# Combined weights of the output projection made on VectorE during the attention heads, and their raw buffers opened earlier

## The chip, the core and the metric

The kernel runs on one core of one Trainium2 chip. A core has a matrix engine (TensorE, PE in the profile, with its weight loads in a row of their own, PEld), a vector engine (VectorE, DVE), an activation engine (ScalarE, ACT), a general engine (GpSimd, POOL) and a queue engine (SyncE, SP), which in this kernel issues nearly all DMAs. Each engine runs its own instructions strictly in the order in which the program lists them; engines wait for one another through semaphores, and a DMA is waited for in the same way. The metric is the device time of one execution in microseconds: the median of three runs of the kernel before is 2246.56 us (2246.27 to 2248.82).

## What is computed

One decoder layer for 1024 prompt tokens behind 16 meta tokens, and for 8 samples of 4 new tokens, each with 1024 cached tokens in pages of 128. All arithmetic is float32. Cut to what matters here:

```python
h = rms_norm(x, norm_pre_g)
u = h @ w_in                                  # 2048 -> 7184 columns, split:
sq, sk, sv, sg, gq, gk, gv, gg, ga = split(u)
o_sb  = stick_breaking_attention(sq, sk, sv)  # 8 heads of 128
o_gla = gated_linear_attention(gq, gk, gv, log_sigmoid(ga @ w_alpha + b_alpha) / 16)   # 4 heads
mixed = concat([o_sb * silu(sg), rms_norm(o_gla) * silu(gg)])    # 2048 columns
y = x + rms_norm(mixed @ w_out, norm_post_g)
```

The samples go through the same layer; their stick-breaking scores run over the cached keys and values (`cache_k`, `cache_v`, found by `page_table`).

## The kernel before

**Matrix products.** A float32 operand is split into a high part (`act.copy` to the float32r type) and a low part (`vec.tensor_tensor` subtract), and each product is three matmuls: high by high, high by low, low by high. `inproj` (lines 279 to 295) makes one block of 128 columns of `h @ w_in`: eight weight chunks of 256 rows, each a DMA into a raw tile `wr`, a ScalarE cast to `wh` and a VectorE subtraction to `wl` (line 185), in buffers of the pool `wp`, three each; then three ranges of tokens with six matmuls each (lines 289 to 291).

**Order of the work.** The program is written out as one stream of projections. Everything else is cut into generators that a `Weaver` holds (lines 51 to 79): after each token range of a chunk `inproj` calls `W.beat()`, and each generator whose delay is over emits its next piece and says after how many beats it wants to go on. So one projection is 24 beats. The planner of the framework then lists each engine's instructions; those made under `urgent()` (weight chunks, evictions) are put ahead as far as their buffers allow. `spread` (line 389) keeps an instruction behind the latest matmul at the time of its beat.

**The stages,** in the order of time: the norm and transposition of x; eight heads (`head`, line 575: projections v, k, q of each, while `attend` runs the attention of the head before); the low rank projection and gates 0 to 2; four heads of gated linear attention from line 634 on (projections gk, gq and two gv each; `own`, `level`, `inside` and `chunks` beside them) and gates 3 and 4; gates 5 to 13 with the values of the cached tokens; gates 14 and 15 from line 1219 on; the output projection from line 1227 on. From the first head to the end of the linear attention `z_feed` (line 344) runs beside everything: one page of cached keys every second beat, four VectorE instructions `jk<-kp,qb` with an accumulator (line 379) for each.

**The attention chain** of one tile (`attend_tile`, line 490): scores on TensorE, X on VectorE (507), two ScalarE functions, X on VectorE (510), a mask on GpSimd (513) on diagonal tiles, a split on ScalarE and VectorE (487), two cumulative matmuls on TensorE (522, 523), then Y and its split and the product with the values.

**The output projection** is a Strassen-like form: seven products of 1024 by 1024 blocks in place of eight. Four of them (p = 5, 6, 7, 4) need differences of blocks of `w_out`. `weight_forms` (line 395) makes these ahead of time into DRAM tiles `td`: for each of 8 row blocks k and 2 column blocks q it loads four 128x512 tiles `tf` (256 KB each), makes four subtractions on GpSimd (line 405) and stores four tiles. It is spawned at line 946, so it runs beside the linear attention; `tf` has one buffer, in the pool `dk`, which is open from the heads to the end of the linear attention.

The left factors need combined blocks of `mixed` (`md` in DRAM): `early` and `later` (lines 1204 to 1213) load 512 column quarters `a11`, `s3`, `s2` into tiles of the pool `oy`, opened at line 1192 before gate 14, and combine them on GpSimd (1208, 1213); `combined` does others on VectorE (1255, 1257) from raw tiles `fr`. `weights` (line 1282) loads a raw weight tile `wr` from `w_out` or `td`, casts (1295) and subtracts (1296) it into one of four places of the `ring`. Raw tiles `wr` (3 buffers) and `fr` (5) lie in the pool `op`, opened at line 1224, after the pool `wp` of the input weights has been closed at 1223. `gain` (line 1317) loads a broadcast row of `norm_post_g` (256 KB); `step` calls it when a column block begins, and `sample_y` (1363) loads it once more. `load_keep` (1459) prepares the weights of the last product, `finish0` (1382) writes the first half of y and `load_xr` (1394) loads x for the second.

Of the kernel before, what the change touches and what calls it, by code (L numbers as in the profile page):

```python
# [10 lines left out]
F32 = mybir.dt.float32  # L11
# [5 lines left out]
ALU = mybir.AluOpType  # L17
# [3 lines left out]
P = 128  # L21
# [61 lines left out]
def hybrid_step(ctx: ExitStack, tc: tile.TileContext, x_prompt, x_sample, cache_k, cache_v, state_gla,  # L83
# [3 lines left out]
    nc = tc.nc  # L87
# [19 lines left out]
    W = Weaver()  # L107
# [236 lines left out]
    def z_feed(rate):  # L344
# [18 lines left out]
        for n, (h, b, i) in enumerate(pages()):  # L363
# [13 lines left out]
            for t in range(NT):  # L377
                jk = dk.tile([P, P], F32, tag="jk", bufs=2, name=f"jk{b}_{h}_{i}_{t}")
                ins = vec.scalar_tensor_tensor(jk[:], kp[:], 1.0, qbs[h, b][:, t, :], ALU.mult, ALU.mult,  # L379
                                         accum_out=zt[:, t, NPG - 1 - i:NPG - i])  # L380
                if t == 0 and W.mark is not None:
                    tc.add_manual_dep(ins.ins, W.mark.name, NOSYNC, reason="spread")
# [12 lines left out]
    def weight_forms():  # L395
        for k in range(8):
            for q in range(2):
                t = dk.tile([P, 4, 512], F32, tag="tf", bufs=1, name=f"tf{k}_{q}")
                for i, (r, c) in enumerate(((0, 0), (0, 1), (1, 1), (1, 0))):
                    r0, c0 = 1024 * r + k * P, 1024 * c + q * 512  # L400
                    spread(nc.sync.dma_start(t[:, i, :], w_out[0, r0:r0 + P, c0:c0 + 512]))
                    yield 3
                yield 2
                for i, a, b in ((0, 1, 0), (1, 1, 2), (2, 2, 0), (3, 3, 2)):
                    spread(pool.tensor_tensor(t[:, i, :], t[:, a, :], t[:, b, :], ALU.subtract))  # L405
                    yield 1
                for j, i in enumerate((0, 2, 1, 3)):
                    yield 2
                    spread(nc.sync.dma_start(td[j][:, k, q * 512:(q + 1) * 512], t[:, i, :]))
# [30 lines left out]
    with tc.tile_pool(name="sp", bufs=1) as sp, tc.tile_pool(name="sps", bufs=1, space=PSUM) as sps:  # L440
# [184 lines left out]
        W.spawn(z_feed(lambda n: 2), lasting=True)  # L625
        for h in range(HEADS):
            head(h)
# [6 lines left out]
    with tc.tile_pool(name="gp", bufs=1) as gp, tc.tile_pool(name="gps", bufs=1, space=PSUM) as gps:  # L634
# [311 lines left out]
        W.spawn(weight_forms(), 4)  # L946
# [244 lines left out]
    with ExitStack() as out:  # L1191
        oy = out.enter_context(tc.tile_pool(name="oy", bufs=24))

        def ytile(nm):
            return oy.tile([P, 512], F32, tag="y", name=nm)[:]
# [8 lines left out]
        def early(k):  # L1204
            quarter(a11[k], 0, 0, k)
            quarter(s3[k], 1, 0, k)
            yield 2
            pool.tensor_tensor(s3[k], s3[k], a11[k], ALU.subtract)

        def later(k):  # L1210
            quarter(s2[k], 1, 1, k)
            yield 2
            pool.tensor_tensor(s2[k], s2[k], s3[k], ALU.add)
# [23 lines left out]
        def raw(nm):  # L1237
            return op.tile([P, 512], F32, tag="fr", bufs=5, name=nm)
# [43 lines left out]
        def weights(p, q, k, dst=None):  # L1282
            with urgent():
# [4 lines left out]
                r = op.tile([P, 512], F32, tag="wr", bufs=3, name=f"wr{p}{q}_{k}")[:]  # L1288
# [28 lines left out]
        def gain(b):  # L1317
            t = op.tile([P, 512], F32, tag="gpost", bufs=2, name=f"gpost{b}_{next(turn)}")
            nc.sync.dma_start(t[:], norm_post_g[0, b * 512:(b + 1) * 512].partition_broadcast(P))
            return t  # L1320
# [42 lines left out]
        def sample_y(sc, b):  # L1363

            rows = slice(32 * b, 32 * b + 32)
            g_ = gain(b)
# [92 lines left out]
        def load_keep():  # L1459

            keep.extend(slot(REGION["B"][i], f"keep{i}") for i in range(4))
            for k in range(8):
                kept.append(weights(4, 1, k, [keep[k // 2][:, (2 * (k % 2) + i) * 512:(2 * (k % 2) + i + 1) * 512] for i in range(2)]))
                yield 2
# [4 lines left out]
                 (3, 1): lambda: (W.spawn(finish0()), W.spawn(load_keep(), 4), W.spawn(load_xr(), 17))}  # L1469
# [27 lines left out]
def build(arrays_by_name):  # L1497
    import concourse.bacc as bacc
    nc = bacc.Bacc("TRN2", target_bir_lowering=False, num_devices=1, dynamic_dma_scratch_size=1024)
# [18 lines left out]
```

## Time and profile before

| | |
|---|---|
| runs, median of 3 | 2246.56 us |
| profiled execution, device time | 2243.48 us |
| profiled execution, first to last instruction | 2241.8 us |
| TensorE, VectorE, ScalarE, GpSimd busy | 2129.0, 1665.4, 999.7, 200.5 us |
| mean granted TensorE clock | 0.984 |
| DMA bytes | 305.09 MB |

Stages by the trace: the heads from about 56 us, first `z_feed` instruction at 135 us, first subtraction of `weight_forms` at 899.6 us and last store at 1510.4 us, the output projection from 1873 us on. In the profile a "busy" TensorE holds an instruction, whatever its clock; the clock is a row of its own. Idle time of an engine counts only where the end waits for it, so the stages are read one by one, and in each the waits of TensorE first.

### The profile page before, as it was taken

The numbers are of one execution on the slowest core, as the hardware profiler recorded it, in microseconds if no ns is written. First come the engines' busy times: TensorE is split into PE (matmuls) and PEld (weight loads), VectorE is DVE, ScalarE is ACT, GpSimd is POOL, SyncE is SP. The second block draws the span as 40 slices with busy tenths as digits, with TensorE's granted clock in tenths as the row PEclk, the third lists the DMA queues.
The fourth block names the chain that finished last, engine by engine and source line by source line (L and its number), as shares of the span: only waits on it lengthen the run. The fifth ranks groups of instructions, "written<-read, shape, count | busy, mean of one in ns | idle before, by whom it ended". The sixth has DMA issues, their size and how long they took to land. (4 is left out here: it accounts for less than half of the span.)

```text
span 2241.8 us, 43812 instructions
## 1 busy us (share of the span) xinstructions
PE 2129.0 (95%) x12640; PEld 1913.8 (85%) x12640; DVE 1665.4 (74%) x6680; ACT 999.7 (45%) x2568; POOL 200.5 (9%) x380
## 2 busy tenths in 40 slices
PE   5999999999999999899999899999999998999987
PEld 5999999999999989798888888887677786788866
DVE  6367777777777787888788877877899867454565
ACT  7355656556565564225244252344344335342331
POOL 0000010010100000311111201100000021000000
PEclk9999999999999999899999999999999999999999
DMA  6224343343433434455545545455566675342484
GB/s 192 58 75 102 83 108 94 99 106 85 104 99 95 102 92 135 131 143 139 157 123 162 139 126 158 134 169 149 169 197 206 199 223 175 125 148 91 133 269 150
DMA packets 380229, 305.09 MB, mean 136 GB/s; under 512 B 49683, under 2 KB 319955, under 8 KB 379987
## 3 DMA queue, kind: packets, MB, share of 16 engines
q1 hardware_dynamic: 377794, 302.02, 46.8%
q8 instruction: 99, 1.62, 0.3%
q14 instruction: 144, 1.17, 0.2%
q10 hardware_dynamic: 2192, 0.27, 0.1%
HBM read 244.44 MB, written 57.72 MB: 135 GB/s over the span
## 5 line engine op out<-in xcount | busy, mean ns | idle before, releaser
L379 DVE SCALAR_TENSOR_TENSOR jk<-kp,qb 128x128 f32<-128x128 f32 x2048 | 518.9, 303 | 65.1 <-DMA kp<-in_cache_k_dram 60.8
L289 PE MATMUL acc_g<-hT,wh_g 128*128 128x368 f32 (+2 forms) x768 | 259.3, 338 | 1.9 <-ACT gx L434 1.7
L291 PE MATMUL acc_g<-hT,wl_g 128*128 128x368 f32 (+2 forms) x768 | 249.7, 325 | 0.7 <-DVE wl_g L185 0.6
L290 PE MATMUL acc_g<-hT,wh_g 128*128 128x368 f32 (+2 forms) x768 | 250.1, 326 | 0.0
L1432 PE MATMUL b<-ring,f 128*128 128x512 f32 x416 | 165.1, 399 | 15.6 <-ACT ring L1295 5.0
L289 PEld LDWEIGHTS acc_g<-hT,wh_g 128*128 128x128 f32 x768 | 145.4, 189 | 35.9 <-issue 22.9
L379 DVE DVE_READ_ACCUMULATOR jk<-kp,qb 128x1 f32 x2048 | 167.6, 82 | 0.0
L1433 PE MATMUL b<-ring,f 128*128 128x512 f32 x416 | 165.3, 397 | 0.0
L1434 PE MATMUL b<-ring,f 128*128 128x512 f32 x416 | 164.9, 396 | 0.0
L1296 DVE TENSOR_TENSOR ring<-wr,ring 128x512 fp32r<-128x512 f32 x104 | 71.2, 690 | 120.5 <-ACT ring L1295 120.2
L291 PEld LDWEIGHTS acc_g<-hT,wl_g 128*128 128x128 f32 x768 | 145.5, 190 | 6.0 <-issue 4.3
L290 PEld LDWEIGHTS acc_g<-hT,wh_g 128*128 128x128 f32 x768 | 145.8, 190 | 4.6 <-issue 3.9
L1295 ACT CAST ring<-wr 128x512 fp32r<-128x512 f32 x104 | 64.0, 621 | 173.2 <-PE sc L1449 89.8
L405 POOL TENSOR_TENSOR tf<-tf 128x512 f32<-128x512 f32 x64 | 90.6, 1416 | 484.0 <-DMA tf<-in_w_out_dram 206.8
L289 PE MATMUL acc_gv<-hT,wh_gv 128*128 128x384 f32 (+1 forms) x384 | 130.6, 340 | 0.0
L290 PE MATMUL acc_gv<-hT,wh_gv 128*128 128x384 f32 (+1 forms) x384 | 128.2, 334 | 0.0
L291 PE MATMUL acc_gv<-hT,wl_gv 128*128 128x384 f32 (+1 forms) x384 | 127.6, 332 | 0.2 <-DVE wl_gv L185 0.2
L289 PE MATMUL acc_k<-hT,wh_k 128*128 128x378 f32 (+1 forms) x384 | 127.8, 333 | 0.0
L289 PE MATMUL acc_q<-hT,wh_q 128*128 128x368 f32 (+2 forms) x384 | 125.5, 327 | 0.0
L290 PE MATMUL acc_k<-hT,wh_k 128*128 128x378 f32 (+1 forms) x384 | 125.5, 327 | 0.0
L291 PE MATMUL acc_k<-hT,wl_k 128*128 128x378 f32 (+1 forms) x384 | 125.3, 326 | 0.0
L290 PE MATMUL acc_q<-hT,wh_q 128*128 128x368 f32 (+2 forms) x384 | 123.8, 322 | 0.0
(436 smaller groups left out, 5898.5 us busy)
## 6 DMA issues: line engine op xcount, KB each, us to landing
kp<-in_cache_k_dram SPq DMA_DIRECT2D x512, 64.0 KB
vr<-in_cache_v_dram SPq DMA_DIRECT2D x64, 512.0 KB
qb<-qsd SPq DMA_DIRECT2D x64, 256.0 KB
wr_g<-in_w_in_dram SPq DMA_DIRECT2D x128, 128.0 KB
tf<-in_w_out_dram SPq DMA_DIRECT2D x64, 256.0 KB
td<-tf SPq DMA_DIRECT2D x64, 256.0 KB
wr<-td SPq DMA_DIRECT2D x64, 256.0 KB
wr<-in_w_out_dram SPq DMA_DIRECT2D x48, 256.0 KB
```

The lines of the kernel that those rows point to most:

```text
L289: mm(acc[c][:, :n], wh[:, k2, :], hh[k][:, lo:hi], start=(k == 0), stop=False)
L290: mm(acc[c][:, :n], wh[:, k2, :], hl[k][:, lo:hi], start=False, stop=False)
L291: W.mark = mm(acc[c][:, :n], wl[:, k2, :], hh[k][:, lo:hi], start=False, stop=(k == NK - 1)).ins
L379: ins = vec.scalar_tensor_tensor(jk[:], kp[:], 1.0, qbs[h, b][:, t, :], ALU.mult, ALU.mult, accum_out=zt[:, t, NPG - 1 - i:NPG - i])
L405: spread(pool.tensor_tensor(t[:, i, :], t[:, a, :], t[:, b, :], ALU.subtract))
L1295: act.copy(wh, r)
L1296: vec.tensor_tensor(wl, r, wh.bitcast(F32), ALU.subtract)
L1432: mm(bk[:], ah, wh, start=first and k == 0, stop=False, skip_group_check=True)
L1433: mm(bk[:], ah, wl, start=False, stop=False, skip_group_check=True)
L1434: mm(bk[:], al, wh, start=False, stop=last and k == 7, skip_group_check=True)
```

## The change

The combined weights are made by VectorE in place of GpSimd, from the first heads on in place of the linear attention: two generators, one for each column block q, are spawned before the heads with delays of 80 and 110 beats, as `lasting` ones, which `W.flush` does not wait for. The delays within a block are longer: 4 beats between the loads, 12 before the subtractions, 4 between subtractions and 4 between stores, 60 beats for a block in place of 26. `tf` gets a second buffer; `jk`, the discarded product of `z_feed`, gets one in place of two, and the DMA scratch of the program is 256 in place of 1024. The combinations in `early` and `later` go from GpSimd to VectorE. The raw tiles `wr` and `fr` of the output projection move from `op` to `oy`, with four buffers each; a tile of each tag is allocated when `oy` opens, before gate 14. `gpost` has three buffers, and `sample_y` uses the gain that `step` has loaded. `load_keep` starts 1 beat after its cause in place of 4 and goes on every 3 beats in place of 2.

```diff
--- before.py
+++ after.py
@@ -375,7 +375,7 @@
                 zt = dk.tile([P, NT, NPG], F32, tag="zt", name=f"zt{b}_{h}")
             kp = kps.pop((h, b, i))
             for t in range(NT):
-                jk = dk.tile([P, P], F32, tag="jk", bufs=2, name=f"jk{b}_{h}_{i}_{t}")
+                jk = dk.tile([P, P], F32, tag="jk", bufs=1, name=f"jk{b}_{h}_{i}_{t}")
                 ins = vec.scalar_tensor_tensor(jk[:], kp[:], 1.0, qbs[h, b][:, t, :], ALU.mult, ALU.mult,
                                          accum_out=zt[:, t, NPG - 1 - i:NPG - i])
                 if t == 0 and W.mark is not None:
@@ -392,21 +392,20 @@
             tc.add_manual_dep(ins.ins, W.mark.name, NOSYNC, reason="spread")
 
 
-    def weight_forms():
+    def weight_forms(q):
         for k in range(8):
-            for q in range(2):
-                t = dk.tile([P, 4, 512], F32, tag="tf", bufs=1, name=f"tf{k}_{q}")
-                for i, (r, c) in enumerate(((0, 0), (0, 1), (1, 1), (1, 0))):
-                    r0, c0 = 1024 * r + k * P, 1024 * c + q * 512
-                    spread(nc.sync.dma_start(t[:, i, :], w_out[0, r0:r0 + P, c0:c0 + 512]))
-                    yield 3
-                yield 2
-                for i, a, b in ((0, 1, 0), (1, 1, 2), (2, 2, 0), (3, 3, 2)):
-                    spread(pool.tensor_tensor(t[:, i, :], t[:, a, :], t[:, b, :], ALU.subtract))
-                    yield 1
-                for j, i in enumerate((0, 2, 1, 3)):
-                    yield 2
-                    spread(nc.sync.dma_start(td[j][:, k, q * 512:(q + 1) * 512], t[:, i, :]))
+            t = dk.tile([P, 4, 512], F32, tag="tf", bufs=2, name=f"tf{k}_{q}")
+            for i, (r, c) in enumerate(((0, 0), (0, 1), (1, 1), (1, 0))):
+                r0, c0 = 1024 * r + k * P, 1024 * c + q * 512
+                spread(nc.sync.dma_start(t[:, i, :], w_out[0, r0:r0 + P, c0:c0 + 512]))
+                yield 4
+            yield 12
+            for i, a, b in ((0, 1, 0), (1, 1, 2), (2, 2, 0), (3, 3, 2)):
+                spread(vec.tensor_tensor(t[:, i, :], t[:, a, :], t[:, b, :], ALU.subtract))
+                yield 4
+            for j, i in enumerate((0, 2, 1, 3)):
+                spread(nc.sync.dma_start(td[j][:, k, q * 512:(q + 1) * 512], t[:, i, :]))
+                yield 4
 
 
     def gate_rest(g, lo, hi, x):
@@ -623,6 +622,8 @@
             W.spawn(attend(h, qt, kt, V), 2)
 
         W.spawn(z_feed(lambda n: 2), lasting=True)
+        for q in range(2):
+            W.spawn(weight_forms(q), 80 + 30 * q, lasting=True)
         for h in range(HEADS):
             head(h)
         low_rank()
@@ -943,7 +944,6 @@
             cbs[g] = gp.tile([P, T], F32, tag="cb", name=f"cb{g}")
             W.spawn(decay(g, cbs[g]), 1)
 
-        W.spawn(weight_forms(), 4)
         for g in range(GH):
             kt = gp.tile([P, T], F32, tag="k", name=f"gk{g}")
             if g == 0:
@@ -1189,10 +1189,12 @@
             nc.sync.dma_start(small[c][:, k, :], md[8 * c + k][:, SEQ:TOUT])
 
     with ExitStack() as out:
-        oy = out.enter_context(tc.tile_pool(name="oy", bufs=24))
+        oy = out.enter_context(tc.tile_pool(name="oy", bufs=4))
+        for tag in ("wr", "fr"):
+            oy.tile([P, 512], F32, tag=tag, name=f"{tag}_")
 
         def ytile(nm):
-            return oy.tile([P, 512], F32, tag="y", name=nm)[:]
+            return oy.tile([P, 512], F32, tag="y", bufs=24, name=nm)[:]
 
         def quarter(dst, r, c, k):
             nc.sync.dma_start(dst, md[8 * c + k][:, 512 * r:512 * r + 512])
@@ -1205,12 +1207,12 @@
             quarter(a11[k], 0, 0, k)
             quarter(s3[k], 1, 0, k)
             yield 2
-            pool.tensor_tensor(s3[k], s3[k], a11[k], ALU.subtract)
+            vec.tensor_tensor(s3[k], s3[k], a11[k], ALU.subtract)
 
         def later(k):
             quarter(s2[k], 1, 1, k)
             yield 2
-            pool.tensor_tensor(s2[k], s2[k], s3[k], ALU.add)
+            vec.tensor_tensor(s2[k], s2[k], s3[k], ALU.add)
 
         for k in range(8):
             W.spawn(early(k), 2 + 2 * k)
@@ -1235,7 +1237,7 @@
             return slots.tile([P, 2176], F32R, tag=f"s{i}", name=nm)
 
         def raw(nm):
-            return op.tile([P, 512], F32, tag="fr", bufs=5, name=nm)
+            return oy.tile([P, 512], F32, tag="fr", name=nm)
 
         def split(hi, lo, src):
 
@@ -1285,7 +1287,7 @@
                     j = next(turn) % 4
                     dst = [t[:, j * 512:(j + 1) * 512] for t in ring]
                 wh, wl = dst
-                r = op.tile([P, 512], F32, tag="wr", bufs=3, name=f"wr{p}{q}_{k}")[:]
+                r = oy.tile([P, 512], F32, tag="wr", name=f"wr{p}{q}_{k}")[:]
                 if p <= 3:
                     r0, c0 = (1024 if p > 1 else 0) + P * k, (1024 if p == 3 else 0) + 512 * q
                     src = w_out[0, r0:r0 + P, c0:c0 + 512]
@@ -1315,7 +1317,7 @@
         at = itertools.count()
 
         def gain(b):
-            t = op.tile([P, 512], F32, tag="gpost", bufs=2, name=f"gpost{b}_{next(turn)}")
+            t = op.tile([P, 512], F32, tag="gpost", bufs=3, name=f"gpost{b}_{next(turn)}")
             nc.sync.dma_start(t[:], norm_post_g[0, b * 512:(b + 1) * 512].partition_broadcast(P))
             return t
 
@@ -1363,7 +1365,7 @@
         def sample_y(sc, b):
 
             rows = slice(32 * b, 32 * b + 32)
-            g_ = gain(b)
+            g_ = gains[b]
             for f in range(2):
                 fs = slice(f * 256, (f + 1) * 256)
                 t = stage(f"sy{b}_{f}")[:, :256]
@@ -1461,12 +1463,12 @@
             keep.extend(slot(REGION["B"][i], f"keep{i}") for i in range(4))
             for k in range(8):
                 kept.append(weights(4, 1, k, [keep[k // 2][:, (2 * (k % 2) + i) * 512:(2 * (k % 2) + i + 1) * 512] for i in range(2)]))
-                yield 2
+                yield 3
 
         kept = []
         AFTER = {(1, 1): lambda: W.spawn(form(5, 2)), (2, 1): lambda: W.spawn(form(3, 2), 8), (6, 1): lambda: W.spawn(form(7, 2)),
                  (5, 1): lambda: W.spawn(form(4, 2)),
-                 (3, 1): lambda: (W.spawn(finish0()), W.spawn(load_keep(), 4), W.spawn(load_xr(), 17))}
+                 (3, 1): lambda: (W.spawn(finish0()), W.spawn(load_keep(), 1), W.spawn(load_xr(), 17))}
         for pair in ((1, 2), (6,), (5, 3), (7, 4)):
             for q in range(2):
                 banks = [bank(f"b{pair[0]}{q}_{t}") for t in range(4)]
@@ -1496,7 +1498,7 @@
 
 def build(arrays_by_name):
     import concourse.bacc as bacc
-    nc = bacc.Bacc("TRN2", target_bir_lowering=False, num_devices=1, dynamic_dma_scratch_size=1024)
+    nc = bacc.Bacc("TRN2", target_bir_lowering=False, num_devices=1, dynamic_dma_scratch_size=256)
     arrays, args = {}, []
     for name in _INS:
         a = arrays_by_name[name]
```

## The prediction

> **What bounds the kernel now.** I read the page first, for the engines over the whole span, and the granted clock of the core.
>
> ```profile
> span 2241.8 us, 43812 instructions
> PE 2129.0 (95%) x12640; PEld 1913.8 (85%) x12640; DVE 1665.4 (74%) x6680; ACT 999.7 (45%) x2568; POOL 200.5 (9%) x380
> core 0: 2241.8 us, clock 0.984
> ```
>
> TensorE is busy 95% of the span, so all that a change of the other engines can win is its 113 us without work and what its lowered clock costs. Then the view by windows shows in which stages these lie: the linear attention, the output projection, the heads (columns: length, busy time and instructions of PE, PEld, DVE, ACT, POOL, granted clock, DMA share, GB/s).
>
> ```profile
> 895.00:1482.00 587.00, 537.00 (x3416) 503.97 (x3417) 477.77 (x2341) 211.28 (x625) 101.41 (x99) 0.97 0.50 142
> 1872.00:2242.00 370.00, 345.37 (x1474) 274.38 (x1474) 199.94 (x371) 126.51 (x291) 1.68 (x1) 0.96 0.50 159
> 170.00:820.00 650.00, 648.83 (x3944) 616.91 (x3943) 507.56 (x2645) 376.29 (x952) 57.14 (x189) 1.00 0.38 96
> ```
>
> In the heads (170 to 820 us) TensorE has 1.2 us without work: the stage is TensorE's own time, and nothing beside it matters as long as it stays covered. In the linear attention (895 to 1482) 50.0 us are missing, in the output projection (from 1872) 24.6 us, and in both the clock is below full. The waits of TensorE in these two stages say for whom:
>
> ```profile
> PE P_d L754 <- DVE at L750: 14.8, 4, 7.4
> PE trp_k L839 <- DVE rep_k L838: 5.8, 4, 3.8
> PE otr L872 <- ACT gst L874: 5.5, 7, 2.8
> PE o L925 <- DMA Sb<-in_state_gla_dram: 4.7, 3, 2.9
> PE P L791 <- DVE at L786: 4.0, 1, 4.0
> PE otr L872 <- DVE ow L866: 3.5, 4, 1.6
> ```
>
> The same view, from 1860 us on (each row: us in total, times, the longest):
>
> ```profile
> PE b L1432 <- ACT ring L1295: 5.0, 1, 5.0
> PE b L1432 <- ACT b L1330: 4.3, 1, 4.3
> PE b L1432 <- ACT u L1339: 3.4, 1, 3.4
> PE b L1432 <- DVE y L1357: 2.8, 1, 2.8
> ```
>
> In the linear attention 28.1 us (14.8 + 5.8 + 4.0 + 3.5) end with VectorE. The output projection has four stops, 15.5 us in all.
>
> **Part 1: the combined weights leave the linear attention.** The 64 subtractions on GpSimd, what VectorE did at the same time, two lines of VectorE inside this stage and inside the heads, and the DMAs of the old generator in this stage:
>
> ```profile
> L405 POOL TENSOR_TENSOR tf<-tf x64: 1260/1300/2296, 899.6 to 1481.3; 128x512 f32<-128x512 f32 x64
> 1402.58 4.19 POOL L405 TENSOR_TENSOR tf<-tf 128x512 f32<-128x512 f32 x3 [1.48 <-DMA tf<-in_w_out_dram]
> 1402.65 1.38 DVE L379 SCALAR_TENSOR_TENSOR jk<-kp,qb 128x128 f32<-128x128 f32 x1
> 1404.17 1.48 DVE L185 TENSOR_TENSOR wl_gv<-wr_gv,wh_gv 128x256 fp32r<-128x256 f32 x1
> 1405.57 1.34 DVE L379 SCALAR_TENSOR_TENSOR jk<-kp,qb 128x128 f32<-128x128 f32 x1
> 895.00:1482.00 587.00, 219.49 (x1584) 0.97 0.50 142
> 300.00:700.00 400.00, 151.66 (x1249) 1.00 0.39 98
> 895.00:1482.00 587.00, 60.92 (x131) 0.97 0.50 142
> 300.00:700.00 400.00, 44.12 (x104) 1.00 0.39 98
> tf<-in_w_out_dram SPq DMA_DIRECT2D x64, 256.0 KB
> td<-tf SPq DMA_DIRECT2D x60, 256.0 KB
> ```
>
> While GpSimd subtracts, a VectorE instruction with two inputs in SBUF takes as long as GpSimd does, 1.34 to 1.48 us. The four rows by windows price this (line 379 in the linear attention and in the heads, then line 185). Line 379 (products and accumulators together) costs 151.66 / 1249 = 0.1214 us an instruction in the heads; 1584 of them would be 192.3 us and take 219.49, so 27.2 us are lost. Line 185: 131 x 44.12 / 104 = 55.6, taken 60.92, 5.3 lost. So at least 32.5 us of VectorE go with the GpSimd work, 0.5 us for each of the 64. VectorE is in order, and what stands behind the blocked instructions are the links that TensorE waits for: just before the 4.0 us wait at line 791, the three instructions above lose some 1.1 + 1.1 + 1.1 us. I take 60% of the 28.1 us, 17 us, and about half of the waits for `gst` (behind `ow` on VectorE) and `Sb` (the DMA share of 0.50 falls by the 64 loads and 60 stores of the last rows), 5 us. The clock of 0.97 over 587 us is 17.6 us of lost time, part of it while TensorE stood; with half of the stops gone I take 6. Together **28 us less**. Bounds: 10 (blocked time is replaced by waits of the same chains) and 50 (all stops).
>
> By the Trainium skill ("TensorE: Matmul & The Clock Gate", part 1) about 3.4 us without work halve the clock for at least as long, and the ramp is under 1% of a usual span. The mean clock of this execution, 0.984, is 1.6% of its span, so the measurement is above that rule; by it, counting no clock at all, the forecast would end some 9 us higher.
>
> **Part 2: they enter the heads.** The price of one 128x512 subtraction on VectorE, and the first and last projection of the heads:
>
> ```profile
> L1296 DVE TENSOR_TENSOR ring<-wr,ring 128x512 fp32r<-128x512 f32 x104 | 71.2, 690 | 120.5 <-ACT ring L1295 120.2
> L289 PE MATMUL acc_k<-hT,wh_k x384: 302/335/437, 73.8 to 744.6; 128*128 128x378 f32 x128, 128*128 128x316 f32 x64
> L289 PE MATMUL acc_q<-hT,wh_q x384: 296/332/446, 98.4 to 773.7; 128*128 128x368 f32 x64, 128*128 128x384 f32 x64, 128*128 128x304 f32 x64
> ```
>
> 64 x 0.69 = 44.2 us of VectorE, over 8 blocks x 60 beats. The eight heads are about 552 beats (two projections of 24 for the first, three for the others) from 73.8 to 774 us, 1.27 us a beat; so the blocks run from about 170 to 820 us, and VectorE there goes from 507.6 to 552 of 650 us (85%). The question is whether TensorE stays covered:
>
> ```profile
> PE z L523 <- DVE lo_s L487: 0.8, 2, 0.6
> DVE X L510 <- ACT X L509: 41.1, 64, 1.4
> DVE jk L379 <- DMA kp<-in_cache_k_dram: 22.3, 13, 4.7
> L513 POOL TENSOR_SCALAR_AFFINE_SELECT X<-X x80: 197/293/1033, 125.8 to 848.3; 127x126 f32<-127x126 f32 x48, 33x32 f32<-33x32 f32 x8, 127x102 f32<-127x102 f32 x8, 25x24 f32<-25x24 f32 x8
> ```
>
> VectorE stands still for its own chain (63.4 us of 695 in the second and third row), which extra work in front shortens only in part; even if none of it shrinks, 552 + 59 is 611 of 650 us, so VectorE is not yet the bound. But the first row says that the attention chain touches its cover already (0.6 us). 64 subtractions of 0.69 us over some 106 tiles delay a tile by 0.4 us on the average; if one tile in six pays it, that is 7 us. Bounds: 0 (all covered) and 60 (second rival). The DMAs move too: 128 issues on SP and 33.5 MB, which bring this stage from 0.38 to about the 0.50 of the linear attention; the loads stand 12 beats (15 us) ahead of their subtraction, a store 4 beats (5 us) behind, so neither holds its queue long, and a second `tf` buffer lets the two blocks alternate. A longer wait for `kp` is in the 7. **7 us more.** One `jk` buffer costs nothing: only VectorE writes it, in order.
>
> The 80 masks of the row above have a median of 0.293 us and a longest of 1.033. By the Trainium skill ("SBUF — State Buffer", who interferes with whom) VectorE with two SBUF inputs and GpSimd reading SBUF exclude each other for a whole instruction, so the moved subtractions would also hold up these masks. GpSimd is busy 57 of 650 us, so by that rule some 6 of the 64 meet one, at most 0.69 us each; with all of it on TensorE's path the sum would be -29 in place of -33.
>
> **Part 3: the output projection.** The first raw weights are waited for by a queue:
>
> ```profile
> SPq L1294 <- PE acc_g L291: 5.1, 1, 5.1
> SPq L1319 <- DVE y L1331: 15.8, 3, 14.0
> ACT keep L1295 <- DMA wr<-td: 16.0, 6, 6.5
> ACT ring L1295 <- DMA wr<-in_w_out_dram: 9.1, 5, 5.0
> ```
>
> SP holds the first `wr` load for 5.1 us until gate 15's last matmul has freed the memory of `wp`; TensorE then stands 5.0 us. In `oy` the tiles are free before gate 14, so the loads and the first casts (the ring lies on columns that gate 15 reads early) go ahead of the end. What is late next is the eviction of gate 15's last accumulator, some 1 us: 4 us less, and 2 for the clock. The stop of 3.4 us is ScalarE's copy `u` behind a ring cast that waits 5.0 us for `wr`; a fourth buffer asks for it one chunk earlier, about 3 us: 2.5 less. The stops of 2.8 and 4.3 us stand among the `keep` weights, the stores of the first half and the loads of x; there a fourth buffer, four fewer `gpost` loads (SP stands 15.8 us for their buffers) and the slower `load_keep` help, but a full DMA queue stays: 3 of 7.1 less, and 0.5 for the clock. **12 us less**, bounds 3 and 18. The 16 combinations that go from GpSimd to VectorE (0.69 us each) stand beside gates 14 and 15; VectorE saves blocked time there and may wait for a load, and I count nothing.
>
> **Sum.** -28 + 7 - 12 = -33 us on the profiled execution's 2243.5; the median of the runs is 3.1 us above it and moves alike: 2246.6 - 33 = 2214 us.
>
> **Rivals.** (a) *The stops of the linear attention are chains, not load*. One stop for `at` has no GpSimd work before it:
>
> ```profile
> 1236.72 0.29 PE L754 MATMUL P_d<-gq,gk 128*48 128x48 f32 x2 [2.47 <-DVE at L750]
> 1239.26 1.36 POOL L405 TENSOR_TENSOR tf<-tf 128x512 f32<-128x512 f32 x1 [24.83 <-DMA kp<-in_cache_k_dram]
> ```
>
> If most are of this kind, the stage gives 10: 2246.6 - 10 + 7 - 12 = 2232. For it speaks also that VectorE is idle 19% of the stage; against it the three blocked instructions in a row. (b) *VectorE breaks the cover of the heads*: at 85% the stage is loaded as the linear attention is now (477.8 of 587, 81%), where TensorE loses 8.5% and clock. Place: line 523 behind 487. At the same rate 650 us would lengthen by 650 x 50 / 537 = 61, and the time be 2246.6 + 61 - 28 - 12 = 2268. It decides as slower from 40 us of new waits. Against it: a head's chain has planned beats between its links, the linear attention has few. (c) *The early buffers do nothing*: if SP does not list the loads ahead, or the DMAs are the limit, part 3 gives 1: 2225.
>
> **Chances.** Forecast and its neighbourhood 0.66, (a) 0.14, (b) 0.10, (c) 0.10. The range takes part 1 at 45, part 2 at 3, part 3 at 15 for its low end (2246.6 - 57 = 2190), and reaches up past (a) and (c) to 2244, leaving (b) and little else outside. About 0.2% (4.5 us) is what a measurement of this kernel can tell from no change: faster 0.86 (forecast, (a), (c), less the tails), same 0.05, slower 0.09 (most of (b)).
>
> **What would show it.** In the changed kernel's windows, 895 on: VectorE busy down by 33 us or more, line 379 at 0.121 us an instruction, and the waits of lines 754 and 791 under half. In the heads: 64 subtractions of 0.69 us on VectorE, TensorE waiting for line 487 some 7 us; 40 us would prove (b). At the start of the output projection no wait of SP for line 291, and the first line 1432 within 2 us of gate 15's end. The forecast is wrong if the linear attention keeps its length, or if the clock in the heads leaves 1.00.

## The result, and the profile after

| | before | after |
|---|---|---|
| time, median (lowest to highest; runs) | 2247.14 us (2246.27 to 2248.82; 4) | 2197.84 us (2192.33 to 2200.35; 4) |
| ratio after / before, 95% interval | | 0.9776 [0.9756, 0.9797] |
| the profiled execution, its span | 2243.48, 2241.8 us | 2199.21, 2197.5 us |
| granted clock | 0.984 | 0.991 |

The change saves 49 us. The forecast of 2214 us was faster by 33, with a range from 2190 to 2244: the measured time lies on the side and in the range that were named, and the sum was 16 us short. The page of the changed kernel (engines, clock), then three windows of it: heads, linear attention, output projection (length; busy time and instructions of PE, PEld, DVE, ACT, POOL; granted clock, DMA share, GB/s).

```profile
span 2197.5 us, 43778 instructions
PE 2108.8 (96%) x12640; PEld 1901.4 (87%) x12640; DVE 1724.1 (78%) x6760; ACT 1001.4 (46%) x2568; POOL 86.6 (4%) x300
core 0: 2197.5 us, clock 0.991
170.00:820.00 650.00, 639.80 (x3859) 603.05 (x3857) 568.50 (x2652) 362.96 (x932) 54.23 (x188) 1.00 0.53 145
895.00:1482.00 587.00, 561.09 (x3614) 529.33 (x3612) 483.56 (x2492) 230.95 (x661) 11.40 (x35) 0.99 0.37 97
1839.00:2198.00 359.00, 339.74 (x1474) 269.73 (x1474) 201.72 (x382) 125.79 (x292) 0.00 (x0) 0.98 0.50 154
```

In the same 650 us of the heads TensorE now runs 3859 instructions instead of 3944; in the 587 us of the linear attention 3614 instead of 3416, at a clock of 0.99 instead of 0.97. The heads lost and the linear attention won. VectorE is the surprise: it got 80 subtractions of 0.69 us (55 us) and was rid of GpSimd's blocking, yet its total rose by 59 us, from 1665.4.

TensorE executes the same number of matmuls in both kernels, so the stages can be compared by the start of the first matmul of a projection or product, after minus before, each in its profiled execution. This table holds it for every kernel of the study, in us; the times and ratios at its end are of all runs. Each column is worked out from the matmul starts in the trace, and the columns' starts before are 880.8, 1547.3, 1625.2, 1843.6 and 2206.7 us. Ahead of gate 14 `buffers_only` and `part3_only` differ from the kernel before in nothing but the size of the DMA scratch, and stand at -7 and -3 us at gate 6; the ten runs of `buffers_only` alone spread over 11 us. So a difference of 7 us or less in one execution's linear attention shows nothing by itself. Up to the first `gk` the scatter is smaller: the four kernels with unchanged heads lie within 1 us of the kernel before.

| kernel | first `gk` | gate 6 | gate 8 | gate 15 | last product | median | ratio, 95% |
|---|---|---|---|---|---|---|---|
| after | +16.5 | -20.6 | -31.8 | -32.6 | -44.1 | 2197.84 | 0.9776 [0.9756, 0.9797] |
| jk_one | +5.3 | +17.4 | +19.8 | +20.3 | +20.3 | 2261.39 | 1.0073 [1.0051, 1.0096] |
| jk_two | +18.1 | -31.3 | -45.5 | -47.2 | -56.7 | 2185.18 | 0.9736 [0.9713, 0.9759] |
| forms_two | +17.8 | -31.8 | -45.9 | -46.4 | -45.3 | 2195.10 | 0.9778 [0.9758, 0.9798] |
| part3_only | -0.1 | -3.2 | -3.0 | -3.2 | -14.4 | 2231.18 | 0.9953 [0.9933, 0.9974] |
| buffers_only | -0.5 | -7.1 | -6.8 | -6.5 | -11.3 | 2235.54 | 0.9974 [0.9959, 0.9989] |
| old_no_subs | +0.4 | -40.6 | -40.6 | -41.0 | -42.9 | 2200.62 | 0.9809 [0.9791, 0.9826] |
| vec_in_place | -1.0 | -38.7 | -38.5 | -38.3 | -38.0 | 2205.36 | 0.9824 [0.9805, 0.9844] |
| pool_heads | +31.9 | -18.1 | -32.0 | -31.8 | -42.9 | 2199.96 | 0.9805 [0.9788, 0.9822] |
| heads_no_subs | +15.9 | -36.2 | -50.2 | -50.2 | -62.9 | 2181.74 | 0.9726 [0.9710, 0.9742] |
| heads_small | +8.1 | -44.3 | -58.5 | -57.9 | -68.2 | 2173.60 | 0.9697 [0.9671, 0.9723] |
| late_400 | +6.7 | -40.8 | -55.0 | -54.6 | -66.9 | 2175.53 | 0.9702 [0.9681, 0.9724] |
| late_520 | +2.1 | -46.2 | -60.3 | -57.7 | -69.2 | 2173.01 | 0.9698 [0.9678, 0.9718] |

So the changed kernel loses 16.5 us up to the first `gk`, wins 37.1 up to gate 6, 11.2 more in gates 6 and 7, 0.8 up to gate 15, and 11.5 in the output projection. The waits of TensorE in the linear attention of the changed kernel (us in total, times, the longest):

```profile
PE o L926 <- DMA Sb<-in_state_gla_dram: 9.0, 4, 2.6
PE P_d L755 <- DVE at L751: 5.8, 1, 5.8
PE al L725 <- POOL lv L696: 3.5, 1, 3.5
PE tr_k L851 <- DVE pk L843: 2.8, 4, 0.9
```

Of the four rows that the prediction put down to VectorE (`P_d`, `trp_k`, `P`, `otr` behind `ow`: 28.1 us) the 5.8 us at `P_d` are left; all that ends with VectorE is down from 31.7 to 9.2 us (5.8, 2.8, and 0.6 in rows under half a us). The state load `Sb` ends 9.0 us instead of 4.7 although the DMAs are less loaded there: a chain that was hidden before is now last. Of the waits for ScalarE this one, of the kernel before, has no row left:

```profile
PE trp_v L839 <- ACT gv L855: 2.7, 3, 1.3
```

In the heads of the changed kernel, 120 to 900 us, TensorE waits for this:

```profile
PE acc_ga L310 <- DVE q L616: 4.1, 1, 4.1
PE z L521 <- ACT hi_s L485: 3.6, 6, 1.1
PE z L522 <- DVE lo_s L486: 2.2, 8, 0.6
```

The prediction looked for some 7 us in the last of these rows (its line 487); it is 2.2. From the first `k` projection to the first `gk` TensorE has 11.5 us without work instead of 1.4, and its matmuls are busy 811.8 us instead of 805.6: that makes the 16.5 us.

### The profile page after: what moved, and what is told of

It reads as the page before. It is cut to its first block, busy times and chain, and to the rows that moved or that the text cites. A ratio compares the mean times of both kernels' runs of the same rounds, so it can differ in the third digit from the quotient of the medians.

```text
span 2197.5 us, 43778 instructions
## 1 busy us (share of the span) xinstructions
PE 2108.8 (96%) x12640; PEld 1901.4 (87%) x12640; DVE 1724.1 (78%) x6760; ACT 1001.4 (46%) x2568; POOL 86.6 (4%) x300
## 4 chain that ended last, share of the span: by engine, by line
PE 69%; DVE 14%; DMA 9%; issue 3%; ACT 3%; SPq 1%; POOL 0%; DVEq 0%; ACTq 0%; POOLq 0%
PE acc_g L289 4%; DVE jk L379 4%; PE acc_g L290 4%; PE b L1436 4%; PE b L1434 4%; PE b L1435 4%; PE acc_g L291 4%; DMA kp<-in_cache_k_dram 3%; PE acc_k L289 3%; PE acc_k L290 3%; PE acc_k L291 3%; PE acc_q L289 2%; PE acc_q L290 2%; PE acc_q L291 2%; PE acc_gv L289 2%
## 5 line engine op out<-in xcount | busy, mean ns | idle before, releaser
L379 DVE SCALAR_TENSOR_TENSOR jk<-kp,qb 128x128 f32<-128x128 f32 x2048 | 590.2, 288 | 76.9 <-DMA kp<-in_cache_k_dram 37.9
L1434 PE MATMUL b<-ring,f 128*128 128x512 f32 x416 | 162.7, 391 | 7.0 <-ACT b L1332 4.0
L1435 PE MATMUL b<-ring,f 128*128 128x512 f32 x416 | 163.0, 392 | 0.3 <-DVE ring L1298 0.3
L1436 PE MATMUL b<-ring,f 128*128 128x512 f32 x416 | 163.1, 392 | 0.0
L507 ACT ACTIVATE X<-X 127x512 f32<-127x512 f32 (+4 forms) x112 | 55.0, 491 | 167.3 <-DVE X L506 167.0
```

Source lines behind the costliest of these rows:

```text
L507: act.activation(X, X, AF.Exp)
L1434: mm(bk[:], ah, wh, start=first and k == 0, stop=False, skip_group_check=True)
L1435: mm(bk[:], ah, wl, start=False, stop=False, skip_group_check=True)
L1436: mm(bk[:], al, wh, start=False, stop=last and k == 7, skip_group_check=True)
```

## The experiments

Each kernel is the kernel before, the changed one or `jk_two` with the edits that are named. `forms_two`, `part3_only` and `buffers_only` have the smaller DMA scratch of the change as well; the scratch was not tried alone.

### One `jk` buffer, put in and taken out

`jk_one` is the kernel before with the change's first hunk, `jk_two` the changed kernel without it:

```diff
-                jk = dk.tile([P, P], F32, tag="jk", bufs=2, name=f"jk{b}_{h}_{i}_{t}")
+                jk = dk.tile([P, P], F32, tag="jk", bufs=1, name=f"jk{b}_{h}_{i}_{t}")
```

> The kernel before with one line of the change: one jk buffer in place of two. Theory A (a product now waits for the accumulator read of the product in front of it): two products that stand back to back start 0.333 us apart instead of 0.212 us, in every stage; line 379 by windows near 0.148 us an instruction instead of 0.121; some 1,300 pairs x 0.121 = about 160 us more of VectorE, and 20 to 45 us more of the whole: 2267 to 2292. Theory B, the prediction's sentence (only VectorE writes it, in order, so it costs nothing): within 4.5 us of 2247 and 0.212 us from start to start.

> The changed kernel with two jk buffers again, all else as changed. Theory A: line 379 back to 0.121 us an instruction, the 16.5 us that the heads and gates 0 to 2 lost shrink to 7 or less, the linear attention gains some 10 more: 2170 to 2188. Theory B: the changed kernel's 2198 within 4.5 us, the heads still 16 us late.

Measured: one buffer costs the kernel before 16.5 us (2261.39 against 2244.88 for before in the same group), and its return wins 12.6 us in the changed kernel's profiled span (2197.5 to 2184.9; medians 2197.84 and 2185.18). Line 379 on VectorE, first in the kernel before, then in the changed kernel (start, duration):

```profile
320.59 0.28 DVE L379 SCALAR_TENSOR_TENSOR jk<-kp,qb 128x128 f32<-128x128 f32 x1
320.80 0.08 DVE L379 DVE_READ_ACCUMULATOR jk<-kp,qb 128x1 f32 x1
320.80 0.28 DVE L379 SCALAR_TENSOR_TENSOR jk<-kp,qb 128x128 f32<-128x128 f32 x1
321.01 0.08 DVE L379 DVE_READ_ACCUMULATOR jk<-kp,qb 128x1 f32 x1
321.01 0.28 DVE L379 SCALAR_TENSOR_TENSOR jk<-kp,qb 128x128 f32<-128x128 f32 x1
```

```profile
322.20 0.29 DVE L379 SCALAR_TENSOR_TENSOR jk<-kp,qb 128x128 f32<-128x128 f32 x1
322.42 0.08 DVE L379 DVE_READ_ACCUMULATOR jk<-kp,qb 128x1 f32 x1
322.54 0.29 DVE L379 SCALAR_TENSOR_TENSOR jk<-kp,qb 128x128 f32<-128x128 f32 x1
322.76 0.08 DVE L379 DVE_READ_ACCUMULATOR jk<-kp,qb 128x1 f32 x1
```

Before, a product starts with the accumulator read of the product in front, 0.21 us after it; now it starts 0.04 us after that read has ended, 0.34 us after the product in front. Over the some 340 back-to-back pairs between 300 and 700 us the median step is 0.333 us, with two buffers 0.212. Each product waits on VectorE's own semaphore in both kernels; the times fit a wait for the read in front of it with one buffer, and for the one before that with two. The prediction looked for 0.121 us an instruction at line 379 in the linear attention of the changed kernel; between 907 and 1470 us it is 241.67 / 1634 = 0.148. VectorE's total shows it: 1724.1 us here, 1647.4 in `jk_two`. In the kernel before, one buffer adds 83 us (1665.4 to 1748.4), half of the 160 that were expected. By the Trainium skill ("VectorE: DVE Perf Modes", "The DRAIN you can't avoid") a semaphore between two VectorE instructions costs nothing extra, measured there on copies; for products with an accumulator this trace shows otherwise: the wait costs 0.121 us each time.

Theory A holds, with less than it asked for in all (2267 to 2292) and at another place: up to the first `gk` one buffer costs little (5.3 us in `jk_one`; the changed kernel is no later there than `jk_two`), from there to gate 6 it costs 12.1 and 12.3 us. The heads' 16.5 us are not its doing: in `jk_two` they are 18.1, where 7 or less were expected.

### The two halves of the change, each alone

`forms_two` has only the new `weight_forms` and its start in the heads, `jk` in two buffers; `part3_only` only the hunks of the output projection; `buffers_only` of those only `wr` and `fr` in `oy`.

> The kernel before with the combined weights alone moved to VectorE beside the heads, jk in two buffers, the output projection untouched. Theory A: heads at most 7 us late, linear attention 35 to 50 us shorter, output projection as before: 2247 - 35 to - 45 = 2202 to 2212, and the stops of 5.0 and 3.4 us at line 1432 stay. Theory B (jk is free): what the changed kernel shows without the output projection's 11 us: 2209, heads 16 us late. If the linear attention's stops were chains (the prediction's rival a): 2232 or more.

> The kernel before with the edits of the output projection alone (wr and fr in oy, the 16 combinations on VectorE, gpost and load_keep); combined weights on GpSimd in the linear attention as before. Theory: what the changed kernel shows from its first product on, -11 us: 2236, with the stops of 5.0 and 3.4 us at line 1432 gone and the linear attention unchanged within 2 us. Rival c of the prediction (the early buffers do nothing): 2246.

> The kernel before with wr and fr in oy alone (four and four buffers, opened early); gpost, load_keep and the 16 combinations as before. By the prediction's terms: first load 4 + 2, the stop of 3.4 us 2.5 less: -8.5, with the two late stops (2.8 and 4.3 us) as before: 2235. All of the output projection's edits gave -14. If the combinations on VectorE matter too, less than 6 is gained: 2238 and more.

Measured: the combined weights alone give 2.2%, as much as the whole change with its single `jk` buffer; the output projection's edits alone 0.5%, 11.2 us between gate 15 and the last product. Together they would make 0.9778 x 0.9953 = 0.973, and `jk_two` has 0.9736: the halves add up. `forms_two` was expected at 2202 to 2212 us: its heads are 17.8 us late where 7 at most were named, and it wins 14.1 us in gates 6 and 7 that no expectation had. In the output projection the stops differ from what was expected. First `buffers_only`, then the changed kernel, TensorE's waits there:

```profile
PE b L1434 <- ACT b L1332: 6.2, 1, 6.2
PE b L1434 <- ACT gx L434: 4.2, 2, 3.9
```

```profile
PE b L1434 <- ACT b L1332: 4.0, 2, 3.5
PE acc_g L289 <- ACT gx L433: 2.1, 1, 2.1
PE b L1434 <- ACT gx L433: 1.9, 2, 1.7
PE b L1434 <- ACT ring L1297: 0.7, 1, 0.7
```

With the buffers alone the first products still wait 3.9 us, now for the eviction of gate 15's accumulator; only with the other hunks does that fall to 1.7. The ratio of `buffers_only` is worth 6 us (2 to 9), its profile 4.8 of the 11.2 (-6.5 to -11.3). The buffers alone take away the stop of 3.4 us with the lowered clock behind it: 5.2 us between the starts of the second and the third product, as in `part3_only` and the changed kernel. The rest is with the combinations, `gpost` and `load_keep`, which were not tried apart.

### GpSimd or VectorE, here or there

`vec_in_place` is the kernel before with the subtractions on VectorE:

```diff
-                    spread(pool.tensor_tensor(t[:, i, :], t[:, a, :], t[:, b, :], ALU.subtract))
+                    spread(vec.tensor_tensor(t[:, i, :], t[:, a, :], t[:, b, :], ALU.subtract))
```

`pool_heads` is the same edit backwards in `jk_two`. In `old_no_subs` the line is left out of the kernel before, in `heads_no_subs` (below) out of `jk_two`.

> The kernel before without its 64 GpSimd subtractions; the 64 loads and 64 stores of the combined weights stay in the linear attention (the stored blocks are then raw weights, so that part of the computation is left out). Theory A (GpSimd's subtractions block VectorE, and the stops of TensorE come from that): the linear attention and gates 3 to 6 give what the move alone gave there, some 50 to 60 us: 2245 - 50 to - 60 = 2185 to 2195, waits of lines 754, 791 and 839 from 27 us to under 10. Theory C (it is the 128 transfers beside the state's and the pages' loads): within 12 us of 2245.

> The kernel before with the 64 subtractions on VectorE where they stood, in the linear attention. Theory A with the prediction's price (0.5 us of VectorE lost for each GpSimd subtraction, against 0.69 us each of its own): VectorE is 12 us busier than before, but no link waits 1.3 us at one go: 2235 to 2255. If GpSimd held VectorE for its whole 1.3 us each (83 us), the stage gains some 20: 2225. If only the place matters and not the engine: 2245 and more.

> The changed kernel with two jk buffers and the 64 subtractions on GpSimd, beside the heads. Theory A: VectorE loses at least 0.5 us to each, and the masks of line 513 stand behind 1.3 us of GpSimd's queue: the heads lose as much as with VectorE or more, 18 to 30 us, in all 2185 to 2197. If the heads' cover takes what the linear attention could not: heads under 8 us late, 2175.

Measured: without its subtractions the kernel before comes to gate 6 41 us earlier; with the same 64 subtractions on VectorE, in the same place, 39 us earlier. So 64 x 1.3 us of GpSimd cost TensorE some 40 us, and 64 x 0.69 us of VectorE some 2 to 5 (2205.36 against 2200.62 in all, with ratios whose intervals overlap). The windows of line 379 between 907 and 1470 us in the kernel before, then of the linear attention and of line 379 in `vec_in_place`:

```profile
907.00:1470.00 563.00, 213.22 (x1542) 0.98 0.50 142
```

```profile
895.00:1482.00 587.00, 564.73 (x3615) 530.24 (x3616) 486.88 (x2533) 222.91 (x654) 11.89 (x35) 0.98 0.54 152
907.00:1470.00 563.00, 193.01 (x1614) 0.98 0.54 152
```

VectorE is as busy as in the kernel before (486.88 after 477.77), the DMAs busier (0.54 after 0.50), and TensorE still runs 3615 instructions in the window instead of 3416. What has changed is the time that VectorE needs for the same instructions: line 379 takes 193.01 / 1614 = 0.1196 us instead of 213.22 / 1542 = 0.1383, line 185 takes 0.423 instead of 0.457. Work that queues behind the subtractions on GpSimd itself is not it: TensorE's wait for `lv` on GpSimd is 4.0 us before, 4.4 without the subtractions and 3.8 in `vec_in_place`. Theory C, that the 128 transfers were to blame, falls as the main cause. The mechanism of part 1 is shown; that the whole 1.3 us hurts, not 0.5, is what the expectation's middle case said (2225), and the gain was larger still. Two things fell short of theory A. `old_no_subs` was expected at 2185 to 2195 us, and its waits at lines 754, 791 and 839 under 10. This row of its waits stays, most of the 14.8 us before:

```profile
PE P_d L754 <- DVE at L750: 11.1, 4, 6.6
```

And the move to the heads wins more than the other engine in place: 49.4 us from the first `gk` to gate 6 in `jk_two`, 52.1 in `heads_no_subs`, against 41.0 in `old_no_subs` and 37.7 in `vec_in_place`. So some 10 us may lie with the transfers in the linear attention or with their old order; this is little above the scatter and was not tried apart.

`pool_heads` is the counterpart: GpSimd beside the heads costs 13.8 us more than VectorE does there (+31.9 against +18.1; 18 to 30 were expected). Its rows of TensorE's waits in the heads:

```profile
PE z L522 <- DVE lo_s L486: 7.5, 16, 1.3
PE z L521 <- ACT hi_s L485: 5.1, 5, 2.5
```

Stops of up to 1.3 us behind VectorE, as long as one subtraction on GpSimd: the cover of the heads does not take them either. Here the masks on GpSimd also stand behind the subtractions (ScalarE waits 13.8 us for line 528 on GpSimd instead of 8.8 in `jk_two`); how much each of the two costs was not tried apart.

### What the heads lose

> The changed kernel with two jk buffers, without the 64 VectorE subtractions; loads and stores stay beside the heads (that part of the computation is left out). Theory V (the heads' 18 us come from 44 us more of VectorE): the heads and gates 0 to 2 end within 4 us of the kernel before, 2185 - 14 to - 18 = 2167 to 2171. Theory D (they come from the 128 transfers and their issues on SP): at least 10 us of the 18 stay: 2177 or more.

`heads_small` also cuts the transfers:

```diff
-                spread(nc.sync.dma_start(t[:, i, :], w_out[0, r0:r0 + P, c0:c0 + 512]))
+                spread(nc.sync.dma_start(t[:, i, :64], w_out[0, r0:r0 + P, c0:c0 + 64]))
...
-                spread(nc.sync.dma_start(td[j][:, k, q * 512:(q + 1) * 512], t[:, i, :]))
+                spread(nc.sync.dma_start(td[j][:, k, q * 512:q * 512 + 64], t[:, i, :64]))
```

> The changed kernel with two jk buffers, no subtractions, and each of the 128 transfers beside the heads cut to 64 of its 512 columns (32 KB instead of 256; the output projection reads raw weights in place of the combined ones, so that part of the computation is left out). Theory B (the bytes: page loads and weight loads land late behind 256 KB transfers, VectorE and ScalarE stand for them): the heads and gates 0 to 2 end within 4 us of the kernel before instead of 16 late, VectorE's waits for kp in the heads fall back from 38 to about 28 us, 2182 - 12 = 2170. Theory Q (128 more issues in SP's order): at least 10 of the 16 us stay, 2180.

Measured, at the first `gk`: 18.1 us late in `jk_two`, 15.9 without the subtractions, 8.1 with an eighth of the bytes as well. So VectorE's 44 us cost 2.2, the bytes 7.8, and 8.1 stay with 128 small transfers: theory V falls, and neither B nor Q has all of it. What comes late is not the page load: VectorE's wait for `kp` is 38.5 us without subtractions and still 35.2 with small transfers. In the changed kernel, 16.5 us late, it is even shorter (24.6) than before (28.4). The load of the values that SP has just stored, for which ScalarE waits, could be it. From `jk_two`, `heads_no_subs` and `heads_small`:

```profile
ACT V L478 <- DMA vr<-out_dram: 10.2, 6, 5.2
```

```profile
ACT V L478 <- DMA vr<-out_dram: 8.1, 5, 5.2
```

```profile
ACT V L478 <- DMA vr<-out_dram: 2.4, 2, 1.3
```

The kernel before and `late_520` have no such row. ScalarE stands here with all that is behind it, among it the casts `hi_s` of the attention. In these five the wait ranks as the delay does. In others it does not: the changed kernel has 3.6 us at 16.5 us late, `pool_heads` 4.0 at 31.9, `late_400` 5.6 at 6.7. So it is not shown that this load is what delays the heads; through which wait the bytes act, and what the last 8.1 us consist of (128 issues of some 0.43 us on SP, or the order of its queue), stays open.

### The blocks later: a faster kernel

```diff
-            W.spawn(weight_forms(q), 80 + 30 * q, lasting=True)
+            W.spawn(weight_forms(q), 400 + 30 * q, lasting=True)
```

`late_520` has 520 in place of 400.

> The changed kernel with two jk buffers and the two generators started 320 beats later (400 and 430 instead of 80 and 110), so that more than half of the blocks fall behind the heads, in gates 0 to 2 and the linear attention. If the heads' loss is per block and the linear attention's cost of a block on VectorE is what the in-place kernel shows (38 to 41 us gained instead of 49, so 8 to 11 us for 16 blocks): heads 7 late instead of 18, linear attention 4 to 6 worse, the pairs of dO as in the changed kernel: 2185 - 5 = 2180. If the pairs fall back to the old order, 10 more: 2190.

> As late_400, with the generators started at 520 and 550: the last 50 or so of the heads' 550 beats hold the first loads, gates 0 to 2 and the linear attention the rest. If the heads pay for the transfers beside them and the linear attention pays 2 us for each 8 blocks (as late_400 showed: 47.5 us gained there against 49.4 with all blocks in the heads): heads 1 to 3 late, linear attention 45 gained, in all 2171 to 2176, the same as late_400 or some 3 less. If the linear attention holds as badly with 16 blocks as the in-place kernel (38 gained): 2180; if the pairs of dO fall back as well: 2190.

Measured: 2175.53 and 2173.01 us, 0.9698 [0.9678, 0.9718] of the kernel before for the second; the changed kernel stood at 0.9776 [0.9756, 0.9797], and `jk_two`, which has the same two `jk` buffers, at 0.9736 [0.9713, 0.9759]. So the later start by itself is worth some 0.4%, with intervals that just meet; the rest is `jk`. In `late_520` the subtractions run from 772 to 1390 us. The heads are 2.1 us late instead of 18.1, and the linear attention, with 52 of the 64 subtractions and 100 of the 128 transfers behind its first `gk`, still wins 48.3 us up to gate 6 (-46.2 - 2.1), against 49.4 with none. The stage that GpSimd's subtractions held up takes VectorE's with no loss that the scatter lets one see.

### Gates 6 and 7

Eight of the kernels win 11 to 14 us between gate 6 and gate 8, the others nothing (`jk_one` loses 2.4); no wait of TensorE accounts for it. The matmuls of the sample scan (`dO`, line 1069), 1500 to 1840 us, of the kernel before, the changed kernel and `jk_two`: busy PE, PEld, clock.

```profile
1500.00:1840.00 340.00, 55.42 (x576) 11.44 (x576) 0.99 0.62 189
```

```profile
1500.00:1840.00 340.00, 48.61 (x576) 10.26 (x576) 0.99 0.65 200
```

```profile
1500.00:1840.00 340.00, 44.54 (x576) 9.52 (x576) 0.99 0.66 205
```

The same 576 matmuls take TensorE 6.8 us less in the changed kernel and 10.9 less in `jk_two`. They write 32 partitions each, and four that follow one another, for four different groups of 32, start within 0.01 us. Two places in TensorE's timeline, the first of the kernel before, the second of `jk_two`:

```profile
1556.77 0.62 PE L1069 MATMUL dO<-vr,dA 128*32 128x512 bf16 x2
1557.32 0.43 PE L289 MATMUL acc_g<-hT,wh_g 128*128 128x368 f32 x1
```

```profile
1523.02 0.42 PE L1069 MATMUL dO<-vr,dA 128*32 128x512 bf16 x2
1523.03 0.41 PE L1069 MATMUL dO<-vvr,dA 128*32 128x512 bf16 x1
1523.03 0.61 PE L1069 MATMUL dO<-vv,dA 128*32 128x512 bf16 x2
1523.27 0.41 PE L1069 MATMUL dO<-vvr,dA 128*32 128x512 bf16 x1
1523.27 0.41 PE L1069 MATMUL dO<-vr,dA 128*32 128x512 bf16 x2
1523.61 0.43 PE L289 MATMUL acc_g<-hT,wh_g 128*128 128x368 f32 x1
```

Two of them between gate matmuls take 0.55 us, eight together 0.59. Counted in the trace, the 576 stand in 83 runs in the kernel before, in 69 in the changed kernel, in 64 in `jk_two`, in 90 in `jk_one`. By the Trainium skill ("TensorE: Matmul & The Clock Gate", part 3) matmuls into different column groups run concurrently; the trace agrees, with starts 0.01 us apart. It is the planner's order that differs. `vec_in_place` and `old_no_subs`, with their transfers in the linear attention to its end, have the old 83 runs and win nothing here (55.43 us in the first); the eight that end their blocks earlier have 64 to 69. In gates 6 and 7 alone they take 14.66 us in the changed kernel and 11.15 in `jk_two` instead of 21.58, so the order accounts for some 7 of the 11.2 us and some 10 of the 14.2. In the rest there are six other matmuls that now stand ahead of gate 6 (455 instead of 461 between the two gates) and gate matmuls that take some 3 us less between the shorter breaks. This is read from the traces: no run changed the order alone, and why the planner cuts the runs otherwise was not settled.

## Why the prediction was right, and where it was wrong

- **Part 1, -28.** Mechanism right and shown by `old_no_subs` and `vec_in_place`; mis-sized. Measured -37.1 in the changed kernel, and -49.4 without the single `jk` buffer (`jk_two`). The terms counted 60% of the waits that name VectorE (17), half of those for `gst` and `Sb` (5) and 6 for the clock. With nothing but the subtractions gone (`old_no_subs`) the first come out close: the four rows fall from 28.1 to 12.3 us, `gst` and `Sb` from 10.2 to 4.3. But smaller waits for VectorE and ScalarE went too, such as the 2.7 us of `trp_v` behind `gv` in the changed kernel; there `Sb` took 4.3 us back. The clock gave more: at most 0.016 x 2241.8 = 36 us were lost to it before, 0.009 x 2197.5 = 20 after, some 16 us won over the whole span where the terms have 8.5. VectorE's busy time did not fall by 33 us there but rose (477.77 to 483.56, with 151 instructions more), for the next reason.
- **"One `jk` buffer costs nothing: only VectorE writes it, in order."** The step that failed. It costs 12.6 us in the changed kernel: with one buffer the next product starts after the read in front of it has ended, and no longer together with it. The rate of 0.1214 us an instruction held the hint: 0.243 us for a product and its read is less than the 0.28 us of a product alone.
- **Part 2, +7.** Measured +16.5, and by another cause. The term counted 64 subtractions of 0.69 us that each delay a tile; they cost 2.2 us with two `jk` buffers. The loads and stores were counted as nothing beyond a longer wait for `kp`, since "neither holds its queue long"; they make 16 us, 7.8 of it by their bytes, and through which wait is open. Rival (b) falls: VectorE at 87% (568.50 of 650) did not break the cover, and no 40 us of waits appeared. The rule of the Trainium skill ("SBUF — State Buffer", who interferes with whom) on the masks, by which the sum would have been -29, has at most these 2.2 us to explain; the 80 masks keep their median of 0.29 us.
- **Gates 6 to 15, 0.** Measured -12.0, of which the new order of `dO` accounts for some 7. No step of the prediction speaks of it, so these 12 us are luck; they could only have been read from the planned order of the new kernel. The 16 combinations beside gates 14 and 15, counted as nothing, did no harm there.
- **Part 3, -12.** Measured -11.5, and -11.2 alone. The sum held, not its split: of the 6 for the first load 2.3 came by the start of the second product (-32.6 to -34.9), since the eviction that was named as late next takes 1.7 us and a stop of 2.1 us appeared at gate 15; the stop of 3.4 us gave 5.2 with its clock (-34.9 to -40.1) where 2.5 stood; the late stops 4.0 where 3.5 stood. No wait of SP for line 291 is left, and the first product follows gate 15's last matmul by 1.7 us, as was said. Rival (c) falls.
- **Rival (a)**, stops that are chains and not load, falls for the stage with the 37 to 49 us. For the longest row it was right: `P_d` keeps 11.1 of 14.8 us without any subtraction (`old_no_subs`), 5.8 in the changed kernel.

Two misses nearly cancel by luck, +9.5 for the heads and -9.1 for the linear attention; with -12.0 for the gates and +0.5 for the output projection they make -11.1, and -33 - 11.1 = -44.1 is the profiled result. The medians add 5 us, within the spread of the runs.

## What to carry over

Beside a GpSimd subtraction of 1.3 us VectorE's two-input instructions took up to 1.48 us instead of 0.28 to 0.42, and TensorE waited for what stood behind them. So in this kernel elementwise work beside VectorE's critical chain belonged on VectorE itself, although VectorE was the busier engine: 64 subtractions cost some 40 us of TensorE on GpSimd and under 5 on VectorE. Before a buffer is cut to one, look whether its writer overlaps with itself: an output that nobody reads still cost a wait for every rewrite here. Work that brings transfers has a price of its own beside what its arithmetic costs: the heads, with 1.2 us of idle TensorE, lost 16 us to 128 transfers, while in `late_520` the linear attention took 100 of them with no loss beyond the scatter. What it is that the transfers delay in the heads was not found.

## What the hardware showed that was not expected

A VectorE product of 128x128 with an accumulator starts 0.212 us behind another, and 0.333 us if it starts only after the read of that one. Two 32-column matmuls between matmuls of another shape cost 0.55 us, eight 0.59: 576 of them kept TensorE busy for 55.4 us in 83 runs and for 44.5 us in 64.
